# Chaining sparse attention's score pairs in program order, and gathering expert tokens with one-hot slots

## The chip, the cores and the metric

The kernel runs on one core of a Trainium2 chip. The metric is the device time of one execution in microseconds (us). Times of the unchanged kernel are given as the median of three timed executions; a fourth execution was taken by the hardware profiler, and all rows below come from that one.

The engines are named as the profile names them: PE is the matrix engine (PEld its weight loads, which overlap its products), DVE the vector engine, ACT the scalar engine, POOL the general engine, and SP the engine whose queue issues the transfers from memory. Each engine takes its instructions in the order in which they stand in its queue.

## The reference, cut to what matters

One layer of a hybrid block over 256 tokens of width 1024. Two attention branches are merged by gates and projected; then a mixture of experts (8 groups of 4) is added.

```python
# branch B, sparse attention (8 heads of 64): an indexer scores all keys, each query keeps 64 of them
_, sel = lax.top_k(score, top_k)
s = jnp.einsum('bqhd,bqkhd->bhqk', qi, k_sel) * (DSA_HEAD_DIM ** -0.5)
p = softmax(where(sel_ok, s, NEG));  out = einsum('bhqk,bqkhd->bqhd', p, v_sel)
...
# mixture of experts: top-1 group by group logits, top-2 experts inside it
g_sel = argmax(group_logits);  top_vals, top_idx = lax.top_k(in_group, 2)
for e in range(32):
    hid = silu(h @ w_gate[e]) * (h @ w_up[e])
    out = out + (hid @ w_down[e]) * combine[:, e:e + 1]
```

Here `h` is the RMS-normed hidden state, so every row of it carries a factor 1/root(mean square) of its token, called `r2` in the kernel.

## The kernel before, in words

**Weights.** All weights arrive as slabs of mostly 1 MB through the SP queue, 33 of attention (`w_att`) and 96 of the experts (`w_moe`). A slab goes to a named place in the on-chip memory, and its load waits in the SP queue until the place's last reader is done. The first 24 expert slabs are loaded during attention into places that attention gives up one after the other. From the 25th on, a load waits for the expert slab that used the same place 24 slabs earlier, so the stream of the remaining 72 begins when the first expert product has read slab 0.

**Attention.** Projections split each weight into a high and a low half (ACT makes one, DVE the other) and run three products per piece of 128x512 on PE (lines 301 to 303). The softmax steps of both branches are placed among these projections by a scheduler, which decides the order on PE from its own estimate; `steps` only gives them priority. `attend_pairs` handles sparse attention: `quad` counts two sets of four heads, `j` two blocks of 128 queries. For each (`quad`, `j`) there are two score banks, z = 0 and 1. Bank z takes the heads whose 64 rows lie in partitions 64z to 64z+63. Each bank is opened by a product that puts the selection's mask into it (line 615), then gets six products of 64 rows (`mm3_pair`, line 318). `mm3_pair` is written so that the two banks alternate, but no order is prescribed between them. `select`, which computes the indexer's scores, calls the same helper. Then DVE takes the row maxima (line 623), ACT the exponentials (line 629), DVE normalises (line 634), PE turns the result (line 640) and multiplies it by the values (line 652). Only two score banks exist, so the next pair waits for the exponentials of the last.

**Routing.** After the last projection PE's order is the program's. `logits` multiplies the hidden state by the router (line 829) for two blocks of 128 tokens, t = 0 and 1; `inv_root` makes `r2` (root on ACT line 344, reciprocal on DVE line 349); `chosen(t)` is a chain of nine DVE steps from the logits (line 843) to `sel`, the chosen experts (line 861). A product with a triangle of ones counts places (`cum`, lines 967, 968 and 975), `place_of` and `slots` turn them into a one-hot matrix `P_` (line 877), and `Pr` is `P_` times `r2` (line 880). `gather` (line 895) multiplies the hidden state by `Pr` into the columns of the experts of a group, and `kept_tokens` copies them out (line 900). The products of an expert with its first two slabs are `gate_up` (line 1047), `hidden` transposes and applies silu, `down` and `combine` finish a group. `heat` is a product that only keeps PE busy, `residual` the addition of the layer's input.

Of the kernel before, what the change touches and what calls it, by code (L numbers as in the profile page):

```python
# [78 lines left out]
def block_kernel(ctx: ExitStack, tc: tile.TileContext, a, out, cap=CAP):  # L79
# [97 lines left out]
        slabs.append((a["w_att"][off:off + 128 * n].rearrange("(p n) -> p n", n=n), n))  # L177
    n_att = len(slabs)
    for i in range(NG * PER_GROUP):
        off = i * 128 * 2048  # L180
        slabs.append((a["w_moe"][off:off + 128 * 2048].rearrange("(p n) -> p n", n=2048), 2048))

    ring = [f"G{i}" for i in range(RING)]
# [127 lines left out]

    row_halves = slice(0, 64), slice(64, 128)

    def mm3_pair(both, start, stop):

        for l, r, s0, s1 in ((1, 3, start, False), (1, 4, False, False), (2, 3, False, stop)):
            for ops in both:
                nc.tensor.matmul(ops[0], ops[l], ops[r], start=s0, stop=s1)  # L318

    scr_turn = [0]  # L320

# [240 lines left out]
    def attend(quad, scores, v, oT, op):  # L562
# [38 lines left out]
        evac(oT[:, 0, 2 * quad:2 * quad + 2], oT[:, 1, 2 * quad:2 * quad + 2], o.rearrange("p (c q) -> p c q", c=2), op)  # L601
        yield

    def attend_pairs(quad, v, oT, op):


# [3 lines left out]
        for j in range(2):  # L610
            nk = 128 * (j + 1)
            qs = slice(j * 128, (j + 1) * 128)
            p = [pss()[:, :2 * nk] for _ in range(2)]
            for z in range(2):
                nc.tensor.matmul(p[z].rearrange("p (h k) -> p h k", h=2), ident_r, bc(bias[:, j, :nk], 2), start=True,
                                 stop=False)
            for i in range(2):
                h = 2 * quad + i
                mm3_pair([(p[z][:, i * nk:(i + 1) * nk], qbT[r, 0, h, qs], qbT[r, 1, h, qs], kbT[r, 0, h, :nk],
                           kbT[r, 1, h, :nk]) for z, r in enumerate(row_halves)], False, i == 1)  # L620
# [24 lines left out]
            yield  # L645
# [71 lines left out]
    obT = at("C1", [128, 2, 4, S])  # L717
    B = [attend_pairs(quad, vb, obT, "C1") for quad in range(2)]
    steps(B[0], 2)
    steps(B[1], 1)  # L720
    steps(B[0], 1)
    steps(B[1], 2)


    def project_late(nslabs, lhs, banks, g=None):
# [142 lines left out]
    Pr = wk.tile([128, 2, GRP], F32, tag="P0", name="Pr", bufs=1)  # L868
# [5 lines left out]
    def slots(grp, t, eng):  # L874

        dst = P_[:, grp % 2, t].rearrange("p (e s) -> p e s", e=EPG)
        nc.vector.tensor_tensor(dst, bc(slot, EPG), bc(place[:, t, EPG * grp:EPG * grp + EPG], CAP, axis=2),
                                op=ALU.is_equal)
        yield
        eng.tensor_scalar(Pr[:, t], P_[:, grp % 2, t], r2[:, t:t + 1], None, op0=ALU.mult)  # L880
        yield

    def placed(t, cum):
        place_of(t, cum)
        yield
        yield from slots(0, t, nc.vector)


    tokens = [wk.tile([128, 4, GRP], F32, tag=f"gt{z}", name="tok", bufs=1) for z in range(2)]

    def gather(c, t, p):

        for k in range(4 * c, 4 * c + 4):
            kk = k - 4 * c
            nc.tensor.matmul(p[:, kk * GRP:(kk + 1) * GRP], x2[:, t, k * 128:(k + 1) * 128], Pr[:, t],  # L895
                             start=(t == 0 and kk == 0), stop=(t == 1 and kk == 3))

    def kept_tokens(c, p):

        nc.vector.tensor_mul(tokens[c], p.rearrange("p (k s) -> p k s", k=4), bc(g_ffn[:, 4 * c:4 * c + 4], GRP, axis=2))  # L900

    OA = [[None, None], [None, None]]

# [50 lines left out]

    in_turn(inv_root(ss2[:, 0, 1:2], D, "n20", early[0], r2[:, 0:1], True))
    squared(512, 512, 1, 1)
    kept = turned(4, 4, 1, 4)
    logits(4, 4, 0)
    kept()
    cums = [pt("cum") for _ in range(2)]  # L960
    in_turn(inv_root(ss2[:, 1, 1:2], D, "n21", early[1], r2[:, 1:2], True), chosen(0))
    logits(4, 4, 1)

    residual(0)
    residual(1)
    heat(lgp[0], 6)
    nc.tensor.matmul(cums[0][:, :NE], tri, sel[:, 0], start=True, stop=True)
    nc.tensor.matmul(cums[1][:, :NE], ones, sel[:, 0], start=True, stop=False)
    residual(2)
    residual(3)  # L970
    heat(lgp[0], 5)
# [12 lines left out]
    urgent.close()  # L984


# [45 lines left out]
        return kept  # L1032

    pls, Gss = {}, {}
    quarters = [slice(32 * j, 32 * j + 32) for j in range(4)]

    def gate_up(n, c, w):

# [133 lines left out]
    with in_order, tc.manual_schedule(engines={mybir.EngineType.Activation, mybir.EngineType.DVE}):  # L1172
        for grp in range(NG):
            if grp + 1 < NG:
                for t in range(2):
                    for _ in slots(grp + 1, t, nc.gpsimd):
                        pass
            for e in range(EPG):
# [13 lines left out]
                if n == 0:  # L1192
                    weigh()
                kept()
                if e == 0 and todo:
                    todo.pop(0)()
                if n == 1:
                    for i in range(4, 8):
                        residual(i)
            if grp + 1 < NG:  # L1200
                for c in range(2):
                    p = pss("gx")
                    for t in range(2):
                        gather(c, t, p)
                    kept_tokens(c, p)
            hidden(EPG * grp + EPG - 1)()
            places(grp)()
            if grp == NG - 1:
                break
# [121 lines left out]
```

## Time and profile before

| | |
|---|---|
| median of three executions | 427.56 us (427.43 to 428.58) |
| the profiled execution | 428.7 us, its span on the core 426.9 us |
| PE, PEld busy | 94%, 69% of the span |
| DVE, ACT, POOL busy | 48%, 43%, 6% |
| read from memory | 133.36 MB, 315 GB/s over the span |

The span runs from the first to the last instruction, and the time of an execution is some 2 us more. "Busy" for PE counts from the issue of a product to its modelled end, and products overlap, so 94% doesn't say that PE is at its peak; the distance between the starts of neighbouring products does. In rows of the timeline the columns are start and length in us, engine, line, operation, what is written from what, the shape, and after x how many instructions stand in the row; a bracket tells how long the engine had been idle before and for whom it waited.

### The profile page before, as it was taken

The numbers are of one execution on the slowest core, as the hardware profiler recorded it, in microseconds if no ns is written. First come the engines' busy times: TensorE is split into PE (matmuls) and PEld (weight loads), VectorE is DVE, ScalarE is ACT, GpSimd is POOL, SyncE is SP. The second block draws the span as 40 slices with busy tenths as digits, with TensorE's granted clock in tenths as the row PEclk, the third lists the DMA queues.
The fourth block names the chain that finished last, engine by engine and source line by source line (L and its number), as shares of the span: only waits on it lengthen the run. The fifth ranks groups of instructions, "written<-read, shape, count | busy, mean of one in ns | idle before, by whom it ended". The sixth has DMA issues, their size and how long they took to land.

```text
span 426.9 us, 8162 instructions
## 1 busy us (share of the span) xinstructions
PE 400.3 (94%) x3288; PEld 292.6 (69%) x3288; DVE 205.8 (48%) x546; ACT 185.2 (43%) x403; POOL 27.7 (6%) x30
## 2 busy tenths in 40 slices
PE   7999999999999999999999999999999797788780
PEld 4888887888877787888886757575757373364440
DVE  2889689989857474757572222121213011020023
ACT  3876688578856665565442122221221111111142
POOL 0890000000000000000001010101010001000000
PEclk9999999999999999999999999999999889698996
DMA  7995673648553464978885999999999999999962
GB/s 264 395 338 194 256 296 129 264 164 332 198 188 128 161 253 176 378 284 341 334 321 184 418 421 421 421 418 420 420 421 419 421 419 421 422 418 420 417 253 104
DMA packets 20639, 135.00 MB, mean 316 GB/s; under 512 B 2418, under 2 KB 2930, under 8 KB 5620
## 3 DMA queue, kind: packets, MB, share of 16 engines
q1 hardware_dynamic: 20596, 134.42, 79.3%
q8 instruction: 28, 0.46, 0.4%
q14 instruction: 15, 0.12, 0.1%
HBM read 133.36 MB, written 1.05 MB: 315 GB/s over the span
## 4 chain that ended last, share of the span: by engine, by line
PE 77%; DMA 19%; DVE 2%; issue 0%; ACT 0%; SPq 0%; DVEq 0%
DMA w<-in_w_moe 18%; PE a L301 13%; PE a L302 13%; PE a L303 13%; PE G L1047 9%; PE gx L895 5%; PE Y L1088 5%; PE OA L1102 3%; PE G L1063 3%; PE s L318 2%; PE o L599 1%; DMA x<-in_x 1%; PE t L640 1%; PE t L539 1%; PE o L652 1%; PE t L451 1%
## 5 line engine op out<-in xcount | busy, mean ns | idle before, releaser
L302 PE MATMUL a<-r 128*128 128x512 f32 (+1 forms) x244 | 93.9, 387 | 0.0
L303 PE MATMUL a<-r 128*128 128x512 f32 (+1 forms) x244 | 92.1, 383 | 0.0
L301 PE MATMUL a<-r 128*128 128x512 f32 (+1 forms) x244 | 84.6, 390 | 0.0
L1047 PE MATMUL G<-w,tok 128*32 128x256 f32 x1024 | 71.2, 406 | 11.6 <-DMA w<-in_w_moe 11.4
L297 DVE SCALAR_TENSOR_TENSOR r<-w,ident,r 128x512 fp32r<-128x512 f32 (+2 forms) x79 | 62.4, 803 | 13.1 <-ACT r L297 12.7
L297 ACT ACTIVATE r<-w,ident 128x512 fp32r<-128x512 f32 (+2 forms) x79 | 57.0, 751 | 24.5 <-PE a L303 22.7
L1047 PEld LDWEIGHTS G<-w,tok 128*32 128x32 f32 x1024 | 30.0, 114 | 38.8 <-issue 15.8
L302 PEld LDWEIGHTS a<-r 128*128 128x128 f32 x244 | 45.9, 188 | 8.7 <-DVE r L297 0.3
L301 PEld LDWEIGHTS a<-r 128*128 128x128 f32 x244 | 45.4, 189 | 9.3 <-ACT r L291 0.5
L303 PEld LDWEIGHTS a<-r 128*128 128x128 f32 x244 | 45.8, 188 | 8.1
L1069 DVE TENSOR_TENSOR P<-G,P 128x64 f32<-128x64 f32 x32 | 7.2, 225 | 82.9 <-ACT P L1068 82.9
L1068 ACT ACTIVATE P<-G 128x64 f32<-128x64 f32 x32 | 7.2, 224 | 73.6 <-PE G L1063 73.6
L1088 PE MATMUL Y<-w,P 128*32 128x256 f32 x512 | 31.0, 382 | 2.2 <-DMA w<-in_w_moe 2.2
L1053 ACT COPY Gs<-G 128x256 f32<-128x256 f32 x32 | 11.9, 372 | 48.8 <-PE G L1047 48.8
L895 PEld LDWEIGHTS gx<-Pr,x 128*128 128x128 f32 x256 | 29.2, 192 | 3.3 <-issue 2.9
L297 DVE SCALAR_TENSOR_TENSOR ysb<-Y,ws,ysb 128x512 fp32r<-128x512 f32 (+1 forms) x18 | 12.5, 692 | 38.8 <-ACT ysb L297 19.6
L895 PE MATMUL gx<-Pr,x 128*128 128x128 f32 x256 | 30.7, 278 | 0.2 <-DVE Pr L880 0.2
L283 DVE TENSOR_TENSOR r<-w,r 128x512 fp32r<-128x512 f32 x32 | 21.9, 690 | 17.3 <-ACT r L282 15.7
L880 POOL TENSOR_SCALAR Pr<-P,r 128x128 f32<-128x128 f32 x14 | 8.3, 606 | 320.2 <-PE gx L895 195.1
L282 ACT CAST r<-w 128x512 fp32r<-128x512 f32 x32 | 19.8, 622 | 15.0 <-PE a L303 8.3
L1063 PEld LDWEIGHTS G<-cst,Gs 128*128 128x128 f32 x128 | 17.5, 199 | 9.8 <-issue 5.3
L1088 PEld LDWEIGHTS Y<-w,P 128*32 128x32 f32 x512 | 15.1, 109 | 12.6 <-DMA w<-in_w_moe 2.5
(223 smaller groups left out, 463.0 us busy)
## 6 DMA issues: line engine op xcount, KB each, us to landing
w<-in_w_moe SPq DMA_DIRECT2D x93, 1024.0 KB, 19.8
w<-in_w_att SPq DMA_DIRECT2D x24, 1024.0 KB, 4.9
w<-in_w_moe SPq DMA_DIRECT2D x6, 512.0 KB, 15.0
w<-in_w_att SPq DMA_DIRECT2D x3, 744.0 KB, 8.4
w<-in_w_att SPq DMA_DIRECT2D x2, 512.0 KB, 5.3
out<-r SPq DMA_DIRECT2D x2, 512.0 KB, 3.5
w<-in_w_att SPq DMA_DIRECT2D x1, 768.0 KB, 6.0
w<-in_w_att SPq DMA_DIRECT2D x2, 372.0 KB, 6.0
```

Of the source, the lines that this page charges most:

```text
L282: nc.scalar.copy(hi, src)
L283: nc.vector.tensor_sub(lo, src, hi.bitcast(F32))
L297: return nc.scalar.mul(hi, ps, g), nc.vector.scalar_tensor_tensor(lo, ps, g, hi.bitcast(F32), op0=ALU.mult, op1=ALU.subtract)
L301: i = nc.tensor.matmul(out_, lh, rh, start=start, stop=False)
L302: nc.tensor.matmul(out_, lh, rl, start=False, stop=False)
L303: nc.tensor.matmul(out_, ll, rh, start=False, stop=stop)
L895: nc.tensor.matmul(p[:, kk * GRP:(kk + 1) * GRP], x2[:, t, k * 128:(k + 1) * 128], Pr[:, t], start=(t == 0 and kk == 0), stop=(t == 1 and ...
L1047: nc.tensor.matmul(G[quarters[2 * z + o], :256], tokens[c][:, kk + o, CAP * e:CAP * e + CAP], w[:, (kk + o) * 512 + z * 256:(kk + o) * 512 ...
L1053: nc.scalar.copy(Gs, G[:, :256])
L1063: nc.tensor.matmul(HT[:, f * 64:(f + 1) * 64], Gs[:, f * 128:(f + 1) * 128], fold, start=True, stop=True)
L1088: nc.tensor.matmul(Y[quarters[e]], hT_[:, e, f], wv[:, f, e], start=f == 0, stop=f == 1)
L1102: nc.tensor.matmul(OA[t][h][:, c0:c0 + w], pl[:, t * 128:(t + 1) * 128], v, start=False, stop=grp == NG - 1 and q0 > 0 and v is lo, skip_g ...
```

## The change

Two things change.

**Pairs.** `mm3_pair` can now tie each product behind the one before, and `attend_pairs` uses that: the twelve products of a pair alternate between the banks, behind both masks, and each pair stands behind the last pair of the queue. The second block of quad 1 is asked for before quad 0's last step.

**Gather.** The expert tokens are gathered with `P_` itself, and `Pr` goes. The factor `r2` comes in later: `factors` multiplies `P_` by `r2` on PE, DVE and PE spread the result over the partitions, and the copy of the gate and up products on ACT (line 1053) takes it as its scale. The places and slots of t = 0 move between the third and the fourth step of `chosen(1)`. Tokens of group 0 are copied out by two experts at a time, those of the first half of the rows before the second half is gathered, and the first expert's product with the first half runs between. So the slabs 1 and 2 trade places in the order of use, and the loop starts with the first halves of two experts. Around the routing, products that only heat go from fourteen to two, the logits of t = 0 go ahead of the last transposes of t = 1, and `residual` moves.

```diff
-        off = i * 128 * 2048
+        off = {1: 2, 2: 1}.get(i, i) * 128 * 2048
...
-    def mm3_pair(both, start, stop):
+    def mm3_pair(both, start, stop, behind=None):
         for l, r, s0, s1 in ((1, 3, start, False), (1, 4, False, False), (2, 3, False, stop)):
             for ops in both:
-                nc.tensor.matmul(ops[0], ops[l], ops[r], start=s0, stop=s1)
+                i = nc.tensor.matmul(ops[0], ops[l], ops[r], start=s0, stop=s1)
+                if behind:
+                    after(i, behind)
+                behind = i
+        return behind
...
+                if not z and paired:
+                    after(i_, paired.pop())
...
     steps(B[0], 2)
+    steps(B[1], 2)
+    steps(B[0], 1)
     steps(B[1], 1)
-    steps(B[0], 1)
-    steps(B[1], 2)
...
+    def factors(grp):
+        p = pss("rq")
+        for t in range(2):
+            nc.tensor.matmul(p[:, :1], P_[:, grp % 2, t], r2[:, t:t + 1], start=(t == 0), stop=(t == 1))
+        rd = wk.tile([128, EPG], F32, tag="rd", name="rd")
+        nc.vector.tensor_scalar(rd, own, p[:, :1], None, op0=ALU.mult)
+        def spread():
+            for q in quarters:
+                nc.tensor.matmul(p[q, 4:4 + EPG], rep, rd, start=True, stop=True)
+            rqs[grp] = wk.tile([128, EPG], F32, tag="rq", name="rq")
+            nc.vector.tensor_copy(rqs[grp], p[:, 4:4 + EPG])
+        return spread
...
-        eng.tensor_scalar(Pr[:, t], P_[:, grp % 2, t], r2[:, t:t + 1], None, op0=ALU.mult)
...
-    kept = turned(4, 4, 1, 4)
     logits(4, 4, 0)
-    kept()
+    turned(4, 4, 1, 4)()
...
-    in_turn(chosen(1))
+    chain = chosen(1)
+    for _ in range(3):
+        next(chain)
     in_turn(placed(0, cums[0][:, :NE]))
+    in_turn(chain)
     gx = [pss("gx") for _ in range(2)]
+    gather(0, 0, 0, gx[0])
     nc.tensor.matmul(cums[1][:, :NE], tri, sel[:, 1], start=False, stop=True)
-    heat(lgp[0], 3)
-    gather(0, 0, gx[0])
-    gather(1, 0, gx[1])
+    gather(0, 1, 0, gx[1])
     in_turn(placed(1, cums[1][:, :NE]))
-    gather(0, 1, gx[0])
-    gather(1, 1, gx[1])
-    for c in range(2):
-        kept_tokens(c, gx[c])
+    gather(0, 0, 1, gx[0])
+    for i in range(2):
+        kept_tokens(0, gx[0], 2 * i, 2)
...
-            nc.scalar.copy(Gs, G[:, :256])
+            nc.scalar.mul(Gs, G[:, :256], rqs[n // EPG][:, e:e + 1])
...
+            if grp == 0:
+                gate_up(0, 0, take()[1])
+                gather(0, 1, 1, gx[1])
+                for i in range(2):
+                    kept_tokens(1, gx[1], 2 * i, 2)
+                spread = factors(0)
+                gate_up(1, 0, take()[1])
+                spread()
+                weigh()
+                gate_up(0, 1, take()[1])()
+                kept = gate_up(1, 1, take()[1])
+                hidden(0)()
+                kept()
```

How the order moves is shown at three places. In these rows a name with a number is one buffer; line numbers behind the change are those of the changed kernel.

PE, the first pair of quad 0 before: `s_1297` and `s_1298` are its two score banks, `a_1575` and `a_1576` banks of a projection.

```order
L451 MATMUL t_1277<-ident_85,r_104 128x128 x4
L318 MATMUL s_1297<-r_1257,r_1065 128x128 x6
L301 MATMUL a_1575<-r_1504,r_910 128x512
L302 MATMUL a_1575<-r_1504,r_910 128x512
L301 MATMUL a_1576<-r_1504,r_910 128x512
L302 MATMUL a_1576<-r_1504,r_910 128x512
L615 MATMUL s_1298<-bias_103,ident_r_92 128x256
L318 MATMUL s_1298<-r_1257,r_1065 128x128 x6
```

The same place in the changed kernel:

```order
L302 MATMUL a_1575<-r_1504,r_910 128x512
L303 MATMUL a_1575<-r_1504,r_910 128x512
L302 MATMUL a_1576<-r_1504,r_910 128x512
L303 MATMUL a_1576<-r_1504,r_910 128x512
L622 MATMUL s_1298<-bias_103,ident_r_92 128x256
L319 MATMUL s_1297<-r_1257,r_1065 128x128
L319 MATMUL s_1298<-r_1257,r_1065 128x128
```

The first bank's six products have moved behind the second bank's mask, and the twelve then alternate. In the other three pairs they do the same; in the last one a pair of transposes stands once between them.

PE, the routing of the changed kernel, from the last logits to the second expert's first product: `s_2191` and `s_2225` are the logits of t = 0 and 1, `t_2244` the last transposes, `gx` the gathered tokens (2293 the first half of the rows), `w33` and `w34` the first two slabs.

```order
L939 MATMUL OA_2268<-x_87,ident_85 128x256
L939 MATMUL OA_2279<-x_87,ident_85 128x256 x2
L922 MATMUL gx_2293<-P_2042,x_87 128x128 x4
L1005 MATMUL cum_2252<-sel_2039,cst_90 128x32
L922 MATMUL gx_2294<-P_2042,x_87 128x128 x4
L922 MATMUL gx_2293<-P_2042,x_87 128x128 x4
L1073 MATMUL G_2330<-w33_1935,tok_2045 32x256 x8
L922 MATMUL gx_2294<-P_2042,x_87 128x128 x4
L888 MATMUL rq_2345<-r2_2030,P_2042 128x1 x2
L1073 MATMUL G_2352<-w34_1937,tok_2045 32x256 x8
```

Before, all four gathers stood behind the last count and ahead of the first expert product. Now one stands ahead of the count and one behind the first expert product.

DVE, the second choice before: from its first step to the scaled slots (`Pr`).

```order
L847 SCALAR_TENSOR_TENSOR other_2034,gs_2033<-lg_2031,gm_2032,cst_90 128x8
L850 TENSOR_SCALAR other_2034<-other_2034,gs_2033 128x8
L852 SCALAR_TENSOR_TENSOR el_2035<-other_2034,lg_2031 128x32
L855 MAX m8s_2037<-el_2035 128x8
L857 COPY top_2038<-m8s_2037 128x2
L859 MATCH_REPLACE el2_2036<-top_2038,el_2035 128x32
L861 TENSOR_SCALAR sel_2039<-el2_2036 128x32
L872 SCALAR_TENSOR_TENSOR place_2040<-cum_2250,sel_2039 128x32
L877 TENSOR_TENSOR P_2042<-cst_90,place_2040 128x128 x2
L880 TENSOR_SCALAR Pr_2043<-P_2042,r2_2030 128x128
```

And in the changed kernel:

```order
L857 SCALAR_TENSOR_TENSOR other_2034,gs_2033<-lg_2031,gm_2032,cst_90 128x8
L901 SCALAR_TENSOR_TENSOR place_2040<-cum_2251,sel_2039 128x32
L906 TENSOR_TENSOR P_2042<-cst_90,place_2040 128x128
L860 TENSOR_SCALAR other_2034<-other_2034,gs_2033 128x8
L906 TENSOR_TENSOR P_2042<-cst_90,place_2040 128x128
L862 SCALAR_TENSOR_TENSOR el_2035<-other_2034,lg_2031 128x32
L865 MAX m8s_2037<-el_2035 128x8
L867 COPY top_2038<-m8s_2037 128x2
L869 MATCH_REPLACE el2_2036<-top_2038,el_2035 128x32
L871 TENSOR_SCALAR sel_2039<-el2_2036 128x32
```

The place and the slots of t = 0 have moved into the chain, and the slots of group 1 (the second row of line 906) come with them.

## Rows read from the trace of the kernel before

**Rows 1.** The chain that ended last, in order of time (start, us, what).

```profile
223.22 3.84 PE gx L895 x32
...
328.45 19.94 DMA w<-in_w_moe
```

**Rows 2.** Windows: stretch, busy us and count by engine, granted clock, DMA share, GB/s.

```profile
226.00:227.00 1.00, 1.00 (x13) 0.88 (x11) 0.75 (x3) 0.00 (x0) 0.00 (x0) 1.00 0.00 0
...
260.00:300.00 40.00, 40.00 (x511) 26.63 (x510) 8.62 (x24) 8.27 (x22) 2.38 (x4) 1.00 1.01 420
```

**Rows 3.** Timeline of the SP queue from 228 us.

```profile
228.12 3.64 SPq L215 DMA_DIRECT2D w<-in_w_moe  x4
```

**Rows 4.** Timeline of PE in `select`, which alternates, with the instruction behind.

```profile
59.69 1.33 PE L318 MATMUL s<-r 64*128 64x128 f32 x20
60.95 0.50 PE L301 MATMUL a<-r 128*128 128x512 f32 x1
...
65.49 0.98 PE L318 MATMUL s<-r 64*128 64x256 f32 x12
66.41 0.50 PE L301 MATMUL a<-r 128*128 128x512 f32 x1
```

**Rows 5.** Timeline of PE at the pairs of quad 0, and in a projection.

```profile
124.17 0.88 PE L318 MATMUL s<-r 64*128 64x128 f32 x6
124.98 0.51 PE L301 MATMUL a<-r 128*128 128x512 f32 x1
...
129.31 0.98 PE L318 MATMUL s<-r 64*128 64x256 f32 x6
130.22 0.44 PE L640 MATMUL t<-ident,P 128*128 128x128 f32 x2
...
134.38 0.39 PE L303 MATMUL a<-r 128*128 128x512 f32 x1
134.60 0.39 PE L301 MATMUL a<-r 128*128 128x512 f32 x1
```

**Rows 6.** Groups by line, 116.5 to 169.3 us (busy, mean ns | idle before, releasers).

```profile
L629 ACT ACTIVATE P<-s,nm 128x128 f32<-128x128 f32 (+1 forms) x16 | 6.6, 416 | 6.2 <-DVE nm L623 6.2
...
L623 DVE TENSOR_REDUCE nm<-s 128x2 f32<-128x256 f32 (+1 forms) x8 | 4.4, 555 | 2.9 <-PE s L318 2.8
```

**Rows 7.** Timeline of the routing, all engines.

```profile
217.04 1.92 PE L829 MATMUL s<-early,x2T 128*128 128x40 f32 x16
217.72 0.30 ACT L344 ACTIVATE n21t<-ss,n21v 128x1 f32<-128x1 f32 x1
218.24 0.15 DVE L349 RECIPROCAL r<-n21t 128x1 f32<-128x1 f32 x1
220.03 0.18 DVE L861 TENSOR_SCALAR sel<-el 128x32 f32<-128x32 f32 x1
220.76 1.11 PE L910 MATMUL OA<-x,ident 128*128 128x256 f32 x4
222.09 0.18 DVE L861 TENSOR_SCALAR sel<-el 128x32 f32<-128x32 f32 x1
222.32 0.41 PE L975 MATMUL cum<-sel,cst 128*128 128x32 f32 x2
222.47 0.49 DVE L877 TENSOR_TENSOR P<-cst,place 128x128 f32<-128x128 f32 x2
222.88 0.28 DVE L880 TENSOR_SCALAR Pr<-P,r 128x128 f32<-128x128 f32 x1
226.20 0.69 DVE L900 TENSOR_TENSOR tok<-gx,ident 128x512 f32<-128x512 f32 x1
226.98 2.80 PE L1047 MATMUL G<-w,tok 128*32 128x256 f32 x48
```

**Rows 8.** Windows of 1 us where TensorE's clock falls (columns as in Rows 2).

```profile
335.00:336.00 1.00, 0.00 (x0) 0.00 (x0) 0.00 (x0) 0.04 (x1) 0.00 (x0) 1.00 0.98 410
...
338.00:339.00 1.00, 0.49 (x8) 0.27 (x12) 0.23 (x1) 0.03 (x1) 0.00 (x0) 0.50 1.02 426
```

More of the change, by code (lines that the diff above doesn't have):

```diff
@@ L602, in attend @@
         yield
+    paired = []
     def attend_pairs(quad, v, oT, op):
@@ L614, in attend_pairs @@
             for z in range(2):
-                nc.tensor.matmul(p[z].rearrange("p (h k) -> p h k", h=2), ident_r, bc(bias[:, j, :nk], 2), start=True,
-                                 stop=False)
+                i_ = nc.tensor.matmul(p[z].rearrange("p (h k) -> p h k", h=2), ident_r, bc(bias[:, j, :nk], 2), start=True,
+                                      stop=False)
+                if not z and paired:
+                    after(i_, paired.pop())
             for i in range(2):
                 h = 2 * quad + i
-                mm3_pair([(p[z][:, i * nk:(i + 1) * nk], qbT[r, 0, h, qs], qbT[r, 1, h, qs], kbT[r, 0, h, :nk],
-                           kbT[r, 1, h, :nk]) for z, r in enumerate(row_halves)], False, i == 1)
+                i_ = mm3_pair([(p[z][:, i * nk:(i + 1) * nk], qbT[r, 0, h, qs], qbT[r, 1, h, qs], kbT[r, 0, h, :nk],
+                           kbT[r, 1, h, :nk]) for z, r in enumerate(row_halves)], False, i == 1, i_)
+            paired.append(i_)
             for z in range(2):
@@ L867, in block_kernel, with slots @@
     hT_ = shaped(P_and_hT[:, 4 * GRP:], [128, EPG, 2, CAP])
-    Pr = wk.tile([128, 2, GRP], F32, tag="P0", name="Pr", bufs=1)
+    rep = cp.tile([128, CAP], F32, name="rep")
+    nc.gpsimd.tensor_add(rep, fold[:, :CAP], fold[:, CAP:])
+    rqs = {}
+    quarters = [slice(32 * j, 32 * j + 32) for j in range(4)]
+    def factors(grp):
[10 more added lines that the diff above has]
+        return spread
     def place_of(t, cum):
         nc.vector.scalar_tensor_tensor(place[:, t], cum, 1.0, sel[:, t], op0=ALU.add, op1=ALU.mult)
-    def slots(grp, t, eng):
+    def slots(grp, t):
         dst = P_[:, grp % 2, t].rearrange("p (e s) -> p e s", e=EPG)
@@ L879, in slots @@
         yield
-        eng.tensor_scalar(Pr[:, t], P_[:, grp % 2, t], r2[:, t:t + 1], None, op0=ALU.mult)
-        yield
     def placed(t, cum):
@@ L885, in placed, with gather, kept_tokens @@
         yield
-        yield from slots(0, t, nc.vector)
+        yield from slots(0, t)
     tokens = [wk.tile([128, 4, GRP], F32, tag=f"gt{z}", name="tok", bufs=1) for z in range(2)]
-    def gather(c, t, p):
+    def gather(grp, c, t, p):
         for k in range(4 * c, 4 * c + 4):
             kk = k - 4 * c
-            nc.tensor.matmul(p[:, kk * GRP:(kk + 1) * GRP], x2[:, t, k * 128:(k + 1) * 128], Pr[:, t],
+            nc.tensor.matmul(p[:, kk * GRP:(kk + 1) * GRP], x2[:, t, k * 128:(k + 1) * 128], P_[:, grp % 2, t],
                              start=(t == 0 and kk == 0), stop=(t == 1 and kk == 3))
-    def kept_tokens(c, p):
-        nc.vector.tensor_mul(tokens[c], p.rearrange("p (k s) -> p k s", k=4), bc(g_ffn[:, 4 * c:4 * c + 4], GRP, axis=2))
+    def kept_tokens(c, p, e0=0, n=EPG):
+        es = slice(CAP * e0, CAP * (e0 + n))
+        nc.vector.tensor_mul(tokens[c][:, :, es], p.rearrange("p (k s) -> p k s", k=4)[:, :, es],
+                             bc(g_ffn[:, 4 * c:4 * c + 4], CAP * n, axis=2))
     OA = [[None, None], [None, None]]
@@ L956, in block_kernel @@
     squared(512, 512, 1, 1)
-    kept = turned(4, 4, 1, 4)
     logits(4, 4, 0)
-    kept()
+    turned(4, 4, 1, 4)()
     cums = [pt("cum") for _ in range(2)]
     in_turn(inv_root(ss2[:, 1, 1:2], D, "n21", early[1], r2[:, 1:2], True), chosen(0))
+    residual(0)
     logits(4, 4, 1)
-    residual(0)
-    residual(1)
-    heat(lgp[0], 6)
+    heat(lgp[0], 2)
     nc.tensor.matmul(cums[0][:, :NE], tri, sel[:, 0], start=True, stop=True)
     nc.tensor.matmul(cums[1][:, :NE], ones, sel[:, 0], start=True, stop=False)
-    residual(2)
-    residual(3)
-    heat(lgp[0], 5)
-    in_turn(chosen(1))
+    for i in range(1, 4):
+        residual(i)
+    chain = chosen(1)
+    for _ in range(3):
+        next(chain)
     in_turn(placed(0, cums[0][:, :NE]))
+    in_turn(chain)
     gx = [pss("gx") for _ in range(2)]
+    gather(0, 0, 0, gx[0])
     nc.tensor.matmul(cums[1][:, :NE], tri, sel[:, 1], start=False, stop=True)
-    heat(lgp[0], 3)
-    gather(0, 0, gx[0])
-    gather(1, 0, gx[1])
+    gather(0, 1, 0, gx[1])
     in_turn(placed(1, cums[1][:, :NE]))
-    gather(0, 1, gx[0])
-    gather(1, 1, gx[1])
-    for c in range(2):
-        kept_tokens(c, gx[c])
+    gather(0, 0, 1, gx[0])
+    for i in range(2):
+        kept_tokens(0, gx[0], 2 * i, 2)
     urgent.close()
@@ L1034, in block_kernel @@
     pls, Gss = {}, {}
-    quarters = [slice(32 * j, 32 * j + 32) for j in range(4)]
     def gate_up(n, c, w):
@@ L1175, in block_kernel @@
                 for t in range(2):
-                    for _ in slots(grp + 1, t, nc.gpsimd):
+                    for _ in slots(grp + 1, t):
                         pass
-            for e in range(EPG):
+            if grp == 0:
[11 more added lines that the diff above has]
+                kept()
+                for i in range(4, 8):
+                    residual(i)
+            for e in range(0 if grp else 2, EPG):
                 n = EPG * grp + e
@@ L1191, in block_kernel @@
                     heat(idle_bank, HEAT)
-                if n == 0:
-                    weigh()
                 kept()
@@ L1196, in block_kernel @@
                     todo.pop(0)()
-                if n == 1:
-                    for i in range(4, 8):
-                        residual(i)
             if grp + 1 < NG:
@@ L1203, in block_kernel @@
                     for t in range(2):
-                        gather(c, t, p)
+                        gather(grp + 1, c, t, p)
                     kept_tokens(c, p)
+                spread = factors(grp + 1)
             hidden(EPG * grp + EPG - 1)()
+            if grp + 1 < NG:
+                spread()
             places(grp)()
```

## The prediction

> **What bounds the kernel now.** I began with the chain that ended last. From 328.45 us on it holds only transfers of expert slabs, and before that PE [rows 1]. The windows tell how tight this is: between 260 and 300 us the transfer engines are full at 420 GB/s [rows 2], which for a slab of 1.05 MB is 2.5 us, and 72 slabs, that is 180 us, come behind the 24 that are loaded early. In the window from 226 us the transfer share is 0.00 [rows 2]: all 24 places are full, and the stream stands still until slab 0 has been read. It goes on at 228.12 us [rows 3], just behind the first sixteen products of `gate_up`: 48 of them begin at 226.98 and take 2.80 us [rows 7], so the first sixteen are done at about 227.9. From the restart to the end of the span (426.9 us) it is 198.8 us, set by the stream. So the time is the moment at which slab 0 is read, plus a part that this change hardly touches. What comes sooner before that moment is worth its full length; what is added to PE, ACT or DVE behind it lies under the stream, as long as PE keeps up.
>
> Before that moment two stretches matter. In the attention PE is dense: one 128x512 product starts 0.22 us after the other [rows 5], with rarely a wait, so time on PE counts in full. In the routing, 217 to 223 us, a chain of short DVE steps sets the pace, and `heat` and `residual` fill PE beside it.
>
> **The pairs.** The reader compares two groups. Where `select` alternates the two halves of the rows, 20 products of 64x128 take 60.95 − 59.69 = 1.26 us, 0.063 each, and 12 of 64x256 take 66.41 − 65.49 = 0.92 [rows 4]. In `attend_pairs` six of one bank stand together: 124.98 − 124.17 = 0.81 us for 128 columns, 130.22 − 129.31 = 0.91 for 256 [rows 5]. So products of one half wait for each other, and products of two halves run side by side. Chained, twelve cost 12 × 0.063 = 0.76 instead of 2 × 0.81 = 1.62, and 0.92 instead of 1.82. Each quad has one pair of either kind: 2 × (0.86 + 0.90) = **3.5 us**. The bounds: nothing (all of it lost to waits), and about 4.1, if each of the four fewer interruptions of the projections also saves some 0.15, the excess of a first product's 0.34 us (124.98 to 125.32) over the pitch; I take no credit for that.
>
> What it may cost is a wait for the banks. Both banks of a pair now fill at once, and the next pair needs both free. To free the first takes a maximum of 0.555 us and two exponentials of 0.416 [rows 6], 1.4 us; the second, behind it on DVE and ACT, about 2.2 to 2.9, with a split of the projections between. In the changed order 8 products of 128x512 stand between the end of the first pair and the next mask, then 24, then 23: covers of 8 × 0.22 = 1.8, 5.3 and 5.1 us, with the first mask's own 0.2 before the second bank is wanted. Only the first turnaround is tight, some 0.2 us at most by the middle of these figures; I set it against the saved interruptions, and the term stays 3.5.
>
> The order of use of the weight slabs moves a little with the projections. These loads were long done when used, so I cost that at nothing; were the cover gone, a slab late by one place would cost 2.5 us once.
>
> **The routing and the gather.** I follow the path to the first `gate_up` in the old kernel's clock, as if attention were unchanged.
>
> (a) The logits of t = 0 pass the last transposes. Logits are 1.92 us for two blocks [rows 7], so transposes, the ACT copies of them and the root behind these in ACT's queue come 0.96 later. The root was at 217.72 with 0.30 and the reciprocal at 218.24 [rows 7], a slack of 0.2; the reciprocal stands in DVE's queue ahead of the first choice. `sel` of t = 0 was finished at 220.21 and comes about 0.8 later, at 221.0. Bounds: 0 (the root is scheduled ahead of the copies) and 1.0.
>
> (b) The second choice took 222.27 − 220.21 = 2.06 from the first. It now has a place (some 0.2) and two slots (0.49 [rows 7]) inside: `sel` of t = 1 at 221.0 + 2.06 + 0.7 = 223.8.
>
> (c) Behind it the count takes 0.41 [rows 7], to 224.2; place and one slot about 0.5, to 224.7. Beside them PE runs the first-half gather of t = 0 early (before 223.8, hidden) and the other half behind the count: a quarter of the 3.84 us of 32 products [rows 1], 0.96, from 223.95 to 224.95. Then the gather that the first expert needs, 0.96, to about 225.95. `Pr` (0.28 [rows 7]) is gone.
>
> (d) Copying the tokens took 0.69 for four experts [rows 7]; for two it lies between half of that and all, and I take 0.42, to 226.4. `gate_up` begins at 226.5 and its sixteen products, a third of 2.80 [rows 7], end at 227.5, against 227.9.
>
> So the gather gains about **0.4 us**; with (a) at nothing it would be 1.2 to 1.7, with (a), (b) and (d) at their upper ends −0.5.
>
> The next slab is read after one more gather (0.96), two short products and sixteen of `gate_up` (0.93), some 2.1 us behind the first. That is less than the 2.5 us of a slab, so the stream should not stop again. Slots on DVE instead of POOL, the product of `P_` with `r2`, its spreading and the scaled copy on ACT fall behind the restart, under a stream that PE outruns: it is PE's turn on the chain until about 328 us, but only through places freed, and from there it is transfers alone [rows 1]. Some 0.3 us of short instructions per group of twelve slabs (30 us of transfers) is no bound; without that cover, eight groups would be 2.4 us.
>
> **The sum.** 3.5 + 0.4 = 3.9. The profiled execution took 428.7 us with a span of 426.9, which I expect at 423.0; it was 1.1 above the median of 427.56. On the median: **423.6 us**.
>
> **Rivals.**
>
> *Waits at the turnarounds eat the pairs' gain.* For it: two score banks, and a maximum and exponentials that stand among other DVE and ACT work. If each of the three turnarounds waits 1.0 to 1.2 us, the gain shrinks by 3.0 to 3.6 and the time is 426.6 to 427.2; with one waiting, 424.4 to 424.8. Against it: covers of 5 us at two of three. Partly 14%, nearly all 6%. [...]
>
> *The clock falls in the routing.* Fourteen heating products become two, so PE stands idle for about 1 us before the first `sel` and 0.5 before the second. [...] From the first `sel` to slab 0's last product PE has about 6.0 us of work (counts 0.5, residuals 1.4, three gathers 2.9, count 0.3, `gate_up` 0.9). At half the clock that doubles: slab 0 is read at 233.6 instead of 227.5, and the time is 427.56 − 3.5 + 5.7 = 429.8. It decides from 3.9 us of doubled work on. Against it: the residuals still lie between, the pauses are shorter than the one in [rows 8], and the clock was 1.00 at 226 us [rows 2]. 5%. [...]
>
> *The routing gives all of its 1.2 to 1.7 us, the interruptions count, or both.* Then 3.5 + 1.2 to 4.1 + 1.7: 421.8 to 422.9. The root may find room ahead of the copies. 13%.
>
> *The pairs don't run side by side, so only the gather counts:* about 427.2. Since [rows 4] shows the same helper with the same operands alternating, 2%.
>
> **How the numbers follow.** The forecast's own case, 422.9 to 424.4, has 60%. About 1.3 us, 0.3%, is what a measurement here can tell from no change. The range from 422.2 to 425.6 leaves out the better part of the routing rival, the full turnarounds, the clock and the pairs that don't overlap, together 2 in 10. Faster by over 0.3% (below 426.3) takes the forecast (60), the partial turnarounds (14) and the routing (13): 0.87. Within 0.3% are the full turnarounds (6) and the pairs alone (2): 0.08. Slower is the clock: 0.05.
>
> **What the profile of the changed kernel will show.** Right: rows of twelve alternating products at line 319 of 0.76 and 0.92 us, and a routing that begins some 3.5 us sooner; no wait of PE for exponentials ahead of the masks at line 622 beyond 0.3 us; the first `w_moe` load of the second round issued near 224.2 instead of 228.12; the reciprocal of t = 1 waiting for ACT's root; granted clock 1.00 between 210 and 230 us; a full stream from there and the same 199 us to the end. Wrong: a hole in the stream behind its restart, which would mean that the second slab is read late; idle time of PE at line 622; a clock of 0.50 in the routing; or more than 199 us behind the restart, which would mean that PE, not the stream, bounds the first groups.

## The result and the profile after

The changed kernel takes 423.81 us (median of five, 423.04 to 425.18) against 427.56 us for the kernel before (median of five, 426.24 to 428.58), a ratio of 0.9904 with a 95% interval from 0.9882 to 0.9926. The profiled execution took 423.63 us with a span of 421.5.

The reading needs three marks on the way to the end: the transposes just ahead of the first pair, the transposes of t = 0 that end the attention and open the routing (called the last transposes from here on), and the restart of the stream. In the kernel before the first two stand here (timeline of PE):

```profile
123.58 0.66 PE L451 MATMUL t<-ident,r 128*128 128x128 f32 x4
...
215.32 0.60 PE L812 MATMUL t<-ident,x 128*128 128x128 f32 x4
```

The changed kernel, timeline of PE, with the pairs of quad 0 between the marks [rows 5]:

```profile
123.16 0.66 PE L456 MATMUL t<-ident,r 128*128 128x128 f32 x4
...
125.16 0.89 PE L319 MATMUL s<-r 64*128 64x128 f32 x12
125.98 0.73 PE L304 MATMUL a<-r 128*128 128x512 f32 x2
...
129.18 0.98 PE L319 MATMUL s<-r 64*128 64x256 f32 x12
130.09 0.50 PE L303 MATMUL a<-r 128*128 128x512 f32 x1
...
210.63 0.60 PE L822 MATMUL t<-ident,x 128*128 128x128 f32 x4
```

Twelve products take 0.82 and 0.91 us where two sixes took 1.62 and 1.82, and no row of line 622 has idle time ahead of it. From mark to mark it is 87.47 us; before it was 91.74.

Its routing, from the timelines of DVE and PE [rows 7]:

```profile
214.30 0.16 DVE L354 RECIPROCAL r<-n21t 128x1 f32<-128x1 f32 x1 [1.01 <-ACT n21t L349]
216.11 0.18 DVE L871 TENSOR_SCALAR sel<-el 128x32 f32<-128x32 f32 x1
218.61 0.18 DVE L871 TENSOR_SCALAR sel<-el 128x32 f32<-128x32 f32 x1
219.25 2.03 PE L922 MATMUL gx<-P,x 128*128 128x128 f32 x16
221.31 0.75 DVE L928 TENSOR_TENSOR tok<-gx,ident 128x256 f32<-128x256 f32 x2 [1.15 <-PE gx L922]
221.79 1.07 PE L1073 MATMUL G<-w,tok 128*32 128x256 f32 x16 [0.52 <-DVE tok L928]
```

DVE waits 1.01 us for the root. Both choices come later, measured from the last transposes (5.66 us to the end of the first `sel`, before 4.89; 8.16 to the second, before 6.95), and what follows the second is shorter: slab 0 is read at 222.86.

The restart (SP queue, answers to [rows 3]), the full stream (windows, answers to [rows 2]) and the chain that ended last (answers to [rows 1]):

```profile
222.92 0.33 SPq L216 DMA_DIRECT2D w<-in_w_moe  x1
```

```profile
240.00:390.00 150.00, 142.50 (x1768) 93.15 (x1767) 29.61 (x93) 30.12 (x72) 0.00 (x0) 0.98 1.01 418
```

```profile
322.95 20.01 DMA w<-in_w_moe
```

The restart has come 5.20 us earlier, the end of the span 5.4. The medians differ by less, 3.75 us, since the profiled execution of before was 1.1 us above its median. The pace of the stream is 418 GB/s where it was 420, and the two streams did not begin alike: in the first 12 us behind the restart the profiled executions of before and of `before_aligned` moved 345 GB/s, the changed kernel 367, the other runs below 359 to 371.

### The profile page after: what moved, and what is told of

It is laid out like the page before. It is cut to its first block, busy times and chain, and to the rows that moved or that the text cites. A ratio compares the mean times of both kernels' runs of the same rounds, so it can differ in the third digit from the quotient of the medians.

```text
span 421.5 us, 8324 instructions
## 1 busy us (share of the span) xinstructions
PE 394.8 (94%) x3372; PEld 291.7 (69%) x3372; DVE 207.5 (49%) x562; ACT 187.3 (44%) x403; POOL 18.9 (4%) x17
## 4 chain that ended last, share of the span: by engine, by line
PE 72%; DMA 20%; DVE 3%; ACT 2%; issue 1%; SPq 0%; DVEq 0%; ACTq 0%
DMA w<-in_w_moe 19%; PE a L302 12%; PE a L303 12%; PE a L304 12%; PE G L1073 9%; PE gx L922 5%; PE Y L1114 4%; PE OA L1128 3%; PE G L1089 2%; PE s L319 2%; DMA w<-in_w_att 1%; PE o L604 1%; PE s L839 1%; PE t L544 1%; DVE tok L928 1%
## 5 line engine op out<-in xcount | busy, mean ns | idle before, releaser
L1073 PE MATMUL G<-w,tok 128*32 128x256 f32 x1024 | 68.1, 394 | 9.9 <-DMA w<-in_w_moe 9.2
L1079 ACT ACTIVATE Gs<-G,rq 128x256 f32<-128x256 f32 x32 | 15.1, 473 | 41.8 <-PE G L1073 41.8
L922 PEld LDWEIGHTS gx<-P,x 128*128 128x128 f32 x256 | 29.4, 192 | 3.5 <-issue 3.5
L922 PE MATMUL gx<-P,x 128*128 128x128 f32 x256 | 31.1, 278 | 0.0
L928 DVE TENSOR_TENSOR tok<-gx,ident 128x512 f32<-128x512 f32 (+1 forms) x18 | 11.2, 631 | 28.9 <-PE gx L922 28.9
```

Of the source, the lines that this page charges most:

```text
L928: nc.vector.tensor_mul(tokens[c][:, :, es], p.rearrange("p (k s) -> p k s", k=4)[:, :, es], bc(g_ffn[:, 4 * c:4 * c + 4], CAP * n, axis=2))
L1073: nc.tensor.matmul(G[quarters[2 * z + o], :256], tokens[c][:, kk + o, CAP * e:CAP * e + CAP], w[:, (kk + o) * 512 + z * 256:(kk + o) * 512 ...
L1079: nc.scalar.mul(Gs, G[:, :256], rqs[n // EPG][:, e:e + 1])
```

## The experiments

All runs in one table. "Attention" is from the first mark to the second, "routing" from there to the restart, "stream" from the restart to the end of the span, all in the profiled execution; the pace is that of 240 to 390 us. The kernel before, timed beside them on the same chips, had medians of 427.67 (the first four runs behind the changed kernel), 427.86 and 427.86 (the next four and the last four).

| run | median, lowest to highest | ratio to before, interval | attention | routing | stream | GB/s |
|---|---|---|---|---|---|---|
| before | 427.56, 426.24 to 428.58 | | 91.74 | 12.80 | 198.8 | 420 |
| changed | 423.81, 423.04 to 425.18 | 0.9904, 0.9882 to 0.9926 | 87.47 | 12.29 | 198.6 | 418 |
| pairs_alone | 423.49, 422.51 to 424.22 | 0.9890, 0.9865 to 0.9914 | 87.41 | 12.81 | 198.1 | 420 |
| gather_alone | 428.36, 427.75 to 429.95 | 1.0010, 0.9991 to 1.0030 | 91.82 | 12.29 | 198.8 | 418 |
| bank_by_bank | 426.20, 424.02 to 427.26 | 0.9949, 0.9929 to 0.9968 | 88.45 | 13.96 | 198.9 | 418 |
| new_steps | 426.79, 426.07 to 428.05 | 0.9977, 0.9962 to 0.9993 | 90.97 | 12.81 | 198.0 | 420 |
| bank_heat | 425.55, 425.35 to 425.69 | 0.9951, 0.9938 to 0.9964 | 88.44 | 12.85 | 198.9 | 418 |
| pairs_shift | 424.66, 423.81 to 425.70 | 0.9930, 0.9914 to 0.9947 | 87.47 | 12.80 | 200.0 | 418 |
| aligned | 420.50, 419.83 to 423.19 | 0.9847, 0.9821 to 0.9873 | 87.44 | 12.29 | 195.7 | 425 |
| root_first | 422.58, 421.80 to 423.94 | 0.9883, 0.9865 to 0.9901 | 87.47 | 11.20 | 198.8 | 418 |
| old_places | 423.78, 423.00 to 424.60 | 0.9907, 0.9886 to 0.9927 | 87.38 | 12.30 | 198.4 | 420 |
| before_aligned | 425.53, 424.85 to 426.49 | 0.9943, 0.9924 to 0.9963 | 91.85 | 12.80 | 196.0 | 425 |
| both | 419.53, 419.07 to 420.11 | 0.9805, 0.9786 to 0.9825 | 87.42 | 11.20 | 195.3 | 425 |
| delay_behind | 425.62, 423.16 to 428.04 | 0.9932, 0.9908 to 0.9956 | 87.37 | 15.60 | 199.0 | 418 |

**The parts by themselves.** `pairs_alone` has the first half of the diff on the kernel before, `gather_alone` the second.

> Only the pairs' part of the change; the gather is that of the kernel before. Theory (the two halves of the rows run side by side, and the end follows the moment at which slab 0 is read, one to one): the first load of the second round is issued some 4.3 us earlier than 228.12, and the time is about 423.3 to 424.1 us. Rival (the gather's part carries a good share, as the two gains together in the profiles are 5.2 us): the load is issued 2 to 3 us earlier and the time is 424.6 to 425.6.

> Only the gather's part of the change; the pairs stand as in the kernel before. Theory: the first choice comes 0.8 us later and the rest gives 1.3 back, so slab 0 is read 0.5 us earlier and the time is about 427.1 us (426.6 to 427.6). Rival (the gather carries a good share): 1.5 to 2.5 us, 425 to 426.

The pairs alone give all of the change's gain: 423.49 against 423.81. The gather's own stretch is 0.5 us shorter, as expected, and yet its time is 428.36, not the 427.1 expected: 0.7 above the kernel before, with an interval that includes no change. Two things take more than the 0.5 back. The kernels with the old gather move 420 GB/s, those with the new one 418. And each execution takes longer than its span on the core, by 1.73 to 1.99 us in the runs with the old gather and by 1.99 to 2.29 in those with the new one, on the mean 0.3 us more; what these 0.3 us are no run shows.

**Alternation or order.** The first takes the alternation out of the queue and keeps the rest, the second keeps only the order in which the steps are asked for:

```diff
-            for i in range(2):
-                h = 2 * quad + i
-                i_ = mm3_pair([(p[z][...], ...) for z, r in enumerate(row_halves)], False, i == 1, i_)
+            for z, r in enumerate(row_halves):
+                for i in range(2):
+                    h = 2 * quad + i
+                    i_ = mm3_pair([(p[z][...], ...)], False, i == 1, i_)
```

```diff
     steps(B[0], 2)
+    steps(B[1], 2)
+    steps(B[0], 1)
     steps(B[1], 1)
-    steps(B[0], 1)
-    steps(B[1], 2)
```

> The changed kernel, but of the twelve chained products of a pair the six of one bank stand ahead of the six of the other; everything else of the order stays. Theory (side by side): twelve products take 1.62 and 1.82 us again instead of 0.82 and 0.91, 3.4 us over the four pairs are lost, and the time is 426.8 to 427.4. Rival (the gain is in the other order of the projections and in fewer interruptions, not in alternation): at most 0.9 us is lost, 423.8 to 424.7.

> The kernel before with only the order in which the steps of the two quads are asked for taken from the change; nothing is chained, and seven products of the last pair happen to alternate. Theory: at most the 0.9 us of the attention's gain that twelve side by side do not explain, and some 0.3 from the few that alternate: 426.4 to 427.6. Rival (the order carries the gain): 3 us or more, below 424.6.

`bank_by_bank`, timeline of PE:

```profile
124.61 1.16 PE L319 MATMUL s<-r 64*128 64x128 f32 x12
125.70 0.73 PE L304 MATMUL a<-r 128*128 128x512 f32 x2
...
128.91 1.32 PE L319 MATMUL s<-r 64*128 64x256 f32 x12
130.16 0.50 PE L303 MATMUL a<-r 128*128 128x512 f32 x1
```

Its median of 426.2 lies near the theory's forecast, but the stretches contradict it. The attention is 88.45 us, only 0.98 longer than with alternation. Twelve products of one bank after the other take 1.09 and 1.25 us, not 1.62 and 1.82. The starts of the products show why. These windows hold the products of 64 rows alone and begin just ahead of a group, so the first count, behind PE's busy time, is how many have begun: first a lone six of the kernel before, then the alternating twelve of the changed kernel, then the twelve of `bank_by_bank`.

```profile
124.15:124.43 0.28, 0.27 (x2) 0.27 (x3) 1.00 0.00 0
124.15:124.79 0.64, 0.62 (x6) 0.63 (x6) 1.00 0.00 0
...
125.15:125.79 0.64, 0.63 (x12) 0.63 (x12) 1.00 0.16 38
...
124.60:124.88 0.28, 0.27 (x2) 0.27 (x3) 1.00 0.40 59
124.60:125.24 0.64, 0.63 (x9) 0.63 (x10) 1.00 0.29 64
124.60:125.60 1.00, 0.99 (x12) 0.99 (x12) 1.00 0.50 172
```

Six products of one bank begin within 0.64 us, 0.11 us apart from the second on. In the same 0.64 us twelve begin when the banks alternate, and nine when one bank stands behind the other in the queue. One by one, the starts of a lone six lie at 0, 0.16, 0.28, 0.39, 0.50 and 0.61 us; those of the twelve in `bank_by_bank` are this pattern twice, the second 0.28 us behind the first. So the second bank's products began while the first bank's were still going on: the edit took the alternation out of the queue, but not the overlap of the two halves. (That each engine takes its instructions in the order of its queue, as said above, so does not hold for PE across the two halves: here the second bank's first product began 0.28 us behind the first bank's first, and the first bank's fourth 0.39 us behind it.) The run measures what alternation adds to standing together, and no more. Over the four pairs the groups of 64-row products, each from its first start to the start of the product behind it, take 7.07 us in the kernel before, 4.79 in `bank_by_bank` and 3.76 in the changed kernel.

The rest of the median is in its routing, where TensorE's clock fell (windows; the column behind POOL's is the granted clock):

```profile
216.00:217.00 1.00, 0.17 (x2) 0.20 (x2) 0.86 (x7) 0.01 (x1) 0.00 (x0) 0.99 1.04 442
217.00:218.00 1.00, 1.00 (x5) 1.00 (x5) 0.86 (x7) 0.00 (x0) 0.00 (x0) 0.50 0.89 360
...
219.00:220.00 1.00, 1.00 (x4) 0.82 (x3) 0.26 (x2) 0.00 (x0) 0.00 (x0) 0.50 0.00 0
220.00:221.00 1.00, 1.00 (x9) 0.91 (x8) 0.00 (x0) 0.00 (x0) 0.00 (x0) 0.80 0.00 0
```

PE was busy 0.17 of the microsecond ahead of the fall; then the granted clock is 0.50 instead of 1.00 from 217 to 220 us, and the routing takes 13.96 us instead of 12.29.

`new_steps` gains 0.77 us in the attention and 0.9 in the median, as the theory allowed.

**The clock.** `bank_heat` puts nine heating products back into `bank_by_bank`:

```diff
     logits(4, 4, 1)
-    heat(lgp[0], 2)
+    heat(lgp[0], 6)
...
     for i in range(1, 4):
         residual(i)
+    heat(lgp[0], 5)
     chain = chosen(1)
```

> The run bank_by_bank with nine heating products put back around the residuals of the routing. In its profile TensorE's granted clock was 0.50 from 217 to 220 us, and the routing from the last transposes of the first half (211.07) to the restart of the stream (225.03) took 13.96 us against 12.29 in the changed kernel. Theory (the pause without heat lets the clock fall, and the doubled work is on the path): the clock stays at 1.00, the stretch is 12.2 to 12.6 us and the time 424.3 to 425.0 instead of 426.2. Rival (the clock has nothing to do with it): unchanged, 426 or, with the heat in the way, more.

```profile
216.00:217.00 1.00, 0.55 (x6) 0.25 (x3) 0.86 (x7) 0.25 (x1) 0.00 (x0) 1.00 0.97 328
217.00:218.00 1.00, 0.92 (x6) 0.92 (x7) 0.83 (x6) 0.00 (x0) 0.00 (x0) 1.00 0.99 418
```

The clock stays at 1.00 in the profile, and six executions lie within 0.34 us of each other, where twelve of `bank_by_bank` spread over 3.2. The routing is 12.85, not the 12.2 to 12.6 expected: the heat stands ahead of the first gather, which begins 0.55 us later from the last transposes than in the changed kernel, and so costs about half a microsecond itself. The median falls by 0.65, to 425.55, where 424.3 to 425.0 was expected.

**The pace.** The change adds a constant table, `rep`, of 128 bytes a partition ahead of the 24 slab places, so every place lies 128 bytes higher: 480 bytes behind a multiple of 512, before 352. (These addresses are reckoned from the sizes of the constants; no view shows them, and only the shifts are in the edits.) Four runs move the places, and what is allocated behind the constants, by an unused table and change nothing else. `pairs_shift` adds 128 bytes to `pairs_alone`; `aligned` adds 32 to the changed kernel (then 0 behind the multiple), `old_places` 384 (then 352); `before_aligned` adds 160 to the kernel before (then 0):

```diff
+    pad = cp.tile([128, 8], F32, name="pad")
+    nc.gpsimd.memset(pad, 0.0)
```

> The run pairs_alone with one unused table of 128 bytes a partition added among the constants, as the changed kernel adds one (rep), so that all 24 slab places lie 128 bytes higher in the on-chip memory; nothing reads the table. Kernels with the old gather moved 420 to 421 GB/s in the full stream, those with the new one 417 to 418, which over 165 us is about 1 us. Theory (the pace hangs on the address of the places): 417 to 418 GB/s, the restart as in pairs_alone, and the time 424.0 to 424.5. Rival (the new gather's own instructions, or the general engine's missing ones, slow the stream): 420 to 421 GB/s and 423.5 as before.

> The changed kernel with an unused table of 32 bytes a partition, after which all slab places begin at a multiple of 512 bytes (before the change they began 352 bytes behind one, after it 480). Theory of the address: another pace than 418 GB/s, 420 or above, and a time of 423.0 or less (422 to 423). Rival (the new gather's instructions): 417 to 418 GB/s and 423.8.

> The changed kernel with an unused table of 384 bytes a partition, after which the slab places begin 352 bytes behind a multiple of 512 again, as before the change. Theory (the pace hangs on the address alone, and the gather's part is worth the 0.5 us by which slab 0 is read earlier): 420 to 421 GB/s in the full stream, 198.0 to 198.2 us from the restart to the end, a time of 422.7 to 423.2, which is 0.3 to 0.8 below pairs_alone. Rival (the new gather's instructions slow the stream as well): 418 to 419 GB/s and 423.5 to 423.9.

> The kernel before with an unused table of 160 bytes a partition, after which the slab places begin at a multiple of 512 bytes. Theory of the address: 425 GB/s, the restart where it was, and 198.1 x 420.5 / 425, some 196 us, from there to the end: 425.2 to 425.9. Rival (the aligned places helped only with the changed kernel's order): 420 to 421 GB/s and 427.6 to 427.9.

The windows from 240 to 390 us, last column GB/s, of `pairs_alone` (352):

```profile
240.00:390.00 150.00, 138.81 (x1667) 88.81 (x1660) 27.61 (x75) 27.14 (x71) 7.13 (x12) 0.95 1.01 420
```

of `pairs_shift` (480):

```profile
240.00:390.00 150.00, 137.61 (x1654) 88.28 (x1648) 27.59 (x75) 26.74 (x70) 7.09 (x12) 0.95 1.01 418
```

of `old_places` (352, with the new gather):

```profile
240.00:390.00 150.00, 142.35 (x1770) 93.71 (x1772) 29.50 (x91) 30.17 (x72) 0.00 (x0) 0.98 1.01 420
```

of `aligned` (0):

```profile
240.00:390.00 150.00, 143.73 (x1796) 95.02 (x1798) 29.62 (x92) 30.39 (x73) 0.00 (x0) 0.98 1.01 425
```

and of `before_aligned` (0):

```profile
240.00:390.00 150.00, 138.70 (x1696) 90.85 (x1695) 29.32 (x81) 27.11 (x71) 7.09 (x12) 0.98 1.01 425
```

The pace goes with the address under either gather: 420, 418, 420, 425, 425. The rival, that the new gather's instructions slow the stream, falls. Aligned places take 2.3 us from the kernel before, as expected, and 3.3 from the changed one, where 0.8 to 1.8 was expected. `pairs_shift`, at 424.66, lies just above its 424.0 to 424.5. `old_places` has its pace back, but its median did not follow: three executions lie at 423.0 to 423.2, as expected, three at 424.4 to 424.6. Two of the slower three have the lowest mean granted clocks of the six (0.978 and 0.979, the others 0.982 and 0.983), which fits a fall of the clock as in `bank_by_bank`; the third has 0.983, and what held it up no profile shows.

**The root.** In `root_first` ACT takes the root for t = 1 ahead of the copy of the last transposes:

```diff
     squared(512, 512, 1, 1)
+    root = inv_root(ss2[:, 1, 1:2], D, "n21", early[1], r2[:, 1:2], True)
     logits(4, 4, 0)
...
-    in_turn(inv_root(ss2[:, 1, 1:2], D, "n21", early[1], r2[:, 1:2], True), chosen(0))
+    in_turn(root, chosen(0))
```

> The changed kernel, but the root for t = 1 stands in ACT's queue ahead of the copy of the last transposes instead of behind it. Theory (the reciprocal that waits 1.01 us for this root delays the first choice, and all behind it): the first choice comes 1.0 to 1.4 us earlier, the second 0.7 to 1.2, slab 0 is read that much sooner, and the time is 422.6 to 423.2. Rival (the second choice hangs on the logits of t = 1, which do not move): at most 0.3 us, 423.5 to 423.8.

```profile
213.34 0.16 DVE L354 RECIPROCAL r<-n21t 128x1 f32<-128x1 f32 x1
215.15 0.18 DVE L871 TENSOR_SCALAR sel<-el 128x32 f32<-128x32 f32 x1
217.81 0.18 DVE L871 TENSOR_SCALAR sel<-el 128x32 f32<-128x32 f32 x1
```

The reciprocal no longer waits. From the last transposes (210.77 here) the first choice comes 1.1 us earlier and the second 0.9, the routing is 11.20 us instead of 12.29, and the median falls by 1.2. The rival falls.

**Both together**, `aligned` with `root_first`:

> The changed kernel with the slab places at multiples of 512 bytes and the root for t = 1 ahead of the copy. Theory (one acts ahead of the restart, the other behind it, so they add): 1.0 to 1.2 us from the restart and 3.0 to 3.3 from the pace, 419.2 to 419.7, faster than all others. Rival (the faster stream is held up by PE in the last groups, so that part of the earlier restart is lost): 420.0 to 420.5.

Its restart and its stream:

```profile
222.10 19.40 SPq L216 DMA_DIRECT2D w<-in_w_moe  x9
```

```profile
240.00:390.00 150.00, 142.98 (x1801) 94.11 (x1800) 29.71 (x92) 30.34 (x73) 0.00 (x0) 0.99 1.01 425
```

The gains add: 1.09 us in the routing, 3.3 in the stream, 419.53 us, the fastest kernel of this study, 8.3 us below the one before.

**Work behind the restart.** `delay_behind` puts thirty heating products, 3.3 us of PE in the trace, into group 1:

```diff
+                if grp == 1 and e == 1:
+                    heat(pss("heat"), 30)
```

> The changed kernel with thirty heating products, some 4 us of PE, between the products of the second expert of group 1, behind the restart of the stream. Theory (work behind the restart lies under the stream as long as PE catches up): the chain turns to transfers some 4 us later than 322.95, and the time is 423.4 to 424.2 as in the changed kernel. Rival (PE sets the places free and so sets the stream back): 425 to 428.

The executions fall in two sets, four from 423.16 to 423.92 and six from 425.55 to 428.04, so the median decides nothing. The profile fell into the second set, and shows why for that execution (windows):

```profile
217.00:218.00 1.00, 1.00 (x4) 0.91 (x5) 0.88 (x5) 0.00 (x0) 0.00 (x0) 0.50 0.91 369
...
222.00:223.00 1.00, 1.00 (x6) 1.00 (x6) 0.69 (x3) 0.00 (x0) 0.00 (x0) 0.50 0.00 0
```

Its routing, which is the changed kernel's instruction by instruction, ran at a granted clock of 0.50 from 217 to 223 us and took 15.60 us instead of 12.29. The mean granted clocks of the other executions fit: 0.981 to 0.989 in the first set, 0.975 to 0.982 in the second. Behind the restart it is 199.0 us, 0.4 more than in the changed kernel for 3.3 us of added PE work: most of the delay lies under the stream, as four of the ten times also say. The other sign did not come true: the chain turned to transfers alone at 270.42 us, not some 4 us later than 322.95.

## Why the prediction was right, point by point

**The end follows the restart.** Right. Wherever the pace is 418 to 420, restart and end stay 198.0 to 199.0 us apart, while the restart moves from 221.97 to 228.12; only `pairs_shift`, with a slow first 12 us (359 GB/s), has 200.0.

**The pairs, 3.5 us.** Right in size and in why. The attention became 4.27 us shorter (91.74 to 87.47). The groups of 64-row products give 3.31 of it (7.07 to 3.76), 0.2 less than predicted: twelve of 128 columns cost 0.82, not 0.76, because the price of one was read from a row of twenty, and in the last pair transposes stand inside the group. The mechanism, "products of one half wait for each other, and products of two halves run side by side", is what the starts show: six or twelve in the same 0.64 us. What the prediction did not have is that standing together is enough for most of it. One bank behind the other, the groups already save 2.28 of the 3.31, and alternation adds 1.03. The last 0.96 of the attention lies outside these groups. The order of the steps is the larger part, since `new_steps` alone shortens the attention by 0.77, 0.61 of it outside the groups; the rest may be the interruptions that the prediction named and took no credit for, but no run separates them. The product behind the lone six begins (124.98) 0.20 us after the last of the six, where the distance inside the group is 0.11; the reason for the difference the trace doesn't show.

**Waits at the turnarounds.** Did not come: no idle time stands ahead of line 622. The rival is out.

**The gather, 0.4 us.** Right for the routing, 0.51, but not for the time: the median of `gather_alone` is no lower than that of the kernel before. Step (a) held almost exactly (the first choice 0.77 later, predicted 0.8), and `root_first` shows that it cost 1.1 us in all. Step (b) was too dear: the second choice came 2.50 us behind the first, not 2.76, so the place and the slots cost the chain 0.44 us and not 0.7.

**"Plus a part that this change hardly touches."** This failed. A table of 128 bytes moved all slab places, and 0.5% of a stream of 180 us is 0.9 us (1.2 by the medians of `pairs_shift` and `pairs_alone`). With the 0.3 us outside the span it more than ate the gather's gain: 0.9 + 0.3 - 0.5 is the 0.7 by which the median of `gather_alone` is higher. That the median, 423.81, came out so close to the forecast of 423.6 is in part luck. The attention gave 0.8 us more than predicted, and the restart came at 222.92 instead of 224.2, while the address and the time outside the span took 1.2 us that the prediction had put at nothing.

**The clock.** The rival was put at 5%, and the changed kernel's own profile shows 1.00 throughout the routing. But the same instructions ran at 0.50 in the profile of `delay_behind`, at a cost of 3.3 us, and heat takes the spread from 3.2 us in `bank_by_bank` to 0.34 in `bank_heat`. So it is a thing that happens to some executions of this kernel, not an outcome that decides between two cases. The rival took its half clock from [rows 8]; that it would double 6.0 us of work was an estimate, and the most that a profile shows is the 3.3. How often it strikes the changed kernel itself was not measured; its slowest execution, 425.18, has the lowest mean granted clock of the five (0.978, the others 0.982 to 0.987) and may be one.

**What stays open:** the third of the slower executions of `old_places`; the 0.3 us outside the span; the slow first 12 us of before, `before_aligned` and `pairs_shift`; and the chaining without the new order of the steps, which was not tried.

## What to carry to other kernels

When a stream of transfers ends the kernel, look at where its destinations lie before counting microseconds elsewhere: here 32 bytes of padding were worth 3.3 us, nearly as much as the whole change with its 3.75. When an experiment reorders products, look at when each of them started before giving the difference a cause: in `bank_by_bank` the queue had lost the alternation, but the engine had not lost the overlap, and nine of the twelve products still began within 0.64 us. And where a pause is left without filling work, profile more than one execution, since here the clock fell to 0.50 in the routing of one profile and stayed at 1.00 in another with the same instructions there.

## What the runs showed of the hardware

The pace of a full stream into places of 8 KB a partition was 425 GB/s when they began, by the reckoning above, at a multiple of 512 bytes (`aligned`, `before_aligned`, `both`), 420 at 352 bytes behind one (the kernel before, `pairs_alone`, `old_places`), and 418 at 480 (the changed kernel, `pairs_shift`). By these paces the same bytes take 1.2% longer at 352 than aligned, and 1.7% longer at 480. No view shows the reason, and other addresses were not tried.

Products of 64 rows and 128 columns in one half of the rows began 0.11 us apart from the second on (six within 0.64 us, in the kernel before). When the halves alternate twelve began in that time (the changed kernel), and when the six of the second half stand behind the six of the first nine did, the second half starting 0.28 us behind the first (`bank_by_bank`).

TensorE's granted clock fell from 1.00 to 0.50 in the routing, where PE waits for the choices, in one profiled execution and not in another of the same instructions: 0.50 from 217 to 223 us in the profile of `delay_behind`, 1.00 throughout the routing in that of the changed kernel.
